# Fixed engine orders: evacuations of scores alternate with copies of the next unit's transposes, and GpSimd casts the first q

## The chip, the cores and the metric

One core of one Trainium2 chip. The metric is the device time of one execution in microseconds (us); lower is better. Ratios are the mean time of one kernel's fast runs over the mean of the other's fast runs of the same rounds, so they are not quite the ratio of the medians quoted beside them.

## The reference

```python
def setup_inputs():
    batch, heads, seq, dim = 8, 8, 512, 64     # q and k, float32, normal
def reference(q, k):
    scale = 1.0 / np.sqrt(q.shape[-1])
    return (np.einsum('bhqd,bhkd->bhqk', q, k) * scale).astype(np.float32)
```

Read 16.8 MB, write 67.1 MB. Everything between stays on the chip.

## The kernel before

The kernel works in 4 units of 2 batches. For a unit it loads k and q (one 2 MB transfer each), casts them to bf16, transposes them on PE in 8 tiles of 8 (128x128 blocks), and copies each transposed tile out of PSUM in four copies, tile by tile on VectorE or ScalarE. Then come 8 store tiles: in each, 4 times two matmuls of 512 columns and one evacuation (scaled, float32), alternately on ScalarE and VectorE; then one 2 MB store. The parts that the change touches:

```python
raw_pool = ... bufs=3      # loaded float32
bf_pool  = ... bufs=5      # cast
out_pool = ... bufs=4      # store tiles, 16 KB a partition
tpsum_pool = ... bufs=2    # transposed tiles, PSUM
psum_pool  = ... bufs=3    # scores, PSUM

def evacuate(dst, src):
    nonlocal n_evac
    if n_evac % 2 == 0:
        nc.scalar.mul(out=dst, in_=src, mul=scale)
    else:
        nc.vector.tensor_scalar(out=dst, in0=src, scalar1=scale, ...)
    n_evac += 1

# load_and_cast(v): two halves of k, then of q
                if v > 0:
                    copy = nc.gpsimd.tensor_copy
                else:
                    copy = (nc.vector.tensor_copy, nc.scalar.copy)[s]

# ... transpose(v, kb, qb) emits all 8 transposed tiles; scores(v, n, kT, qz) one store tile ...

cast = [load_and_cast(0)]
clear(nc.vector, qzs[0], 0)
clear(nc.gpsimd, qzs[0], 1)
for h in range(2):
    clear(nc.gpsimd, qzs[1], h)
for v in range(1, UNITS):
    cast.append(load_and_cast(v))

ts = {0: transpose(0, *cast[0])}
for v in range(UNITS):
    for n in range(N):
        scores(v, n, *ts[v])
        if n == (1 if v == 0 else N // 2 - 1) and v + 1 < UNITS:
            ts[v + 1] = transpose(v + 1, *cast[v + 1])
```

Nothing says in which order an engine runs the copies of the next unit and the evacuations of this one: a scheduler decides, and it runs the copies in a burst.

Of the kernel before, what the change touches and what calls it, by code (L numbers as in the profile page):

```python
# [1 line left out]

# [5 lines left out]


@with_exitstack  # L10
def kernel(
    ctx: ExitStack,
    tc: tile.TileContext,
    q: bass.AP,
    k: bass.AP,
    out: bass.AP,
):






    nc = tc.nc
    B, H, S, D = q.shape
    scale = 1.0 / (D ** 0.5)
    P = 128
    UNITS = B // 2
    N = H
    M = P // (2 * H)  # L30
    R = S // M
    J = R // 2
    RO = 8
    U = S // RO
    JJ = J // RO
    IW = 8 // JJ

    f32 = mybir.dt.float32
    bf16 = mybir.dt.bfloat16

    q_r = q.rearrange("(v b) g (m j) d -> v (b g m) (j d)", b=2, j=R)
    k_r = k.rearrange("(v b) g (m j) d -> v (b g m) (j d)", b=2, j=R)
    out_r = out.rearrange("(v b) (n h) (u i) k -> v (b n) (h u) (i k)", b=2, h=2, i=RO)

    consts = ctx.enter_context(tc.tile_pool(name="consts", bufs=1))
    raw_pool = ctx.enter_context(tc.tile_pool(name="raw", bufs=3))
    bf_pool = ctx.enter_context(tc.tile_pool(name="bf", bufs=5))
    t_pool = ctx.enter_context(tc.tile_pool(name="t", bufs=2))
    out_pool = ctx.enter_context(tc.tile_pool(name="out", bufs=4))
    tpsum_pool = ctx.enter_context(tc.tile_pool(name="tpsum", bufs=2, space=bass.MemoryType.PSUM))  # L50
    psum_pool = ctx.enter_context(tc.tile_pool(name="psum", bufs=3, space=bass.MemoryType.PSUM))

    n_evac = 0
    n_tp = 0

    def evacuate(dst, src):
        nonlocal n_evac
        if n_evac % 2 == 0:
            nc.scalar.mul(out=dst, in_=src, mul=scale)  # L59
        else:  # L60
            nc.vector.tensor_scalar(out=dst, in0=src, scalar1=scale, scalar2=None,  # L61
                                    op0=mybir.AluOpType.mult)
        n_evac += 1

    def half(h):
        return slice(h * D, (h + 1) * D)

    def load_and_cast(v):

        both = []  # L70
        for src in (k_r, q_r):
            xf = raw_pool.tile([P, 2, J * D], f32, name="xf")
            nc.sync.dma_start(out=xf, in_=src[v])
            xb = bf_pool.tile([P, J, 2, D], bf16, name="xb")
            for s in range(2):
                if v > 0:
                    copy = nc.gpsimd.tensor_copy
                else:
                    copy = (nc.vector.tensor_copy, nc.scalar.copy)[s]
                copy(out=xb[:, :, s, :], in_=xf[:, s].rearrange("p (j d) -> p j d", j=J))  # L80
            both.append(xb)
        return both

    def clear(engine, qz, h):

        engine.memset(qz[half(h), :, :, (1 - h) * U:(2 - h) * U], 0.0)  # L86

    def rearrange(tp, pattern, dst):

        nonlocal n_tp  # L90
        copy = (nc.vector.tensor_copy, nc.scalar.copy)[n_tp % 2]
        n_tp += 1
        for s in range(2):
            src = tp[half(s)].rearrange(pattern, n=N, h=2)
            for h in range(2):
                copy(out=dst(s, h), in_=src[:, h])  # L96

    def transpose(v, kb, qb):

        kT = t_pool.tile([P, N, M, 2, J], bf16, name="kT")  # L100
        qz = qzs[v % 2]
        for j0 in range(0, J, 8):
            tp = tpsum_pool.tile([P, 8, P], bf16, name="tp")
            for j in range(8):
                nc.tensor.transpose(out=tp[:, j, :], identity=identity,  # L105
                                    in_=kb[:, j0 + j].rearrange("p s d -> p (s d)"))
            rearrange(tp, "d j (n h m) -> d h n m j",
                      lambda s, h: kT[half(h), :, :, s, j0:j0 + 8])
        for i0 in range(0, RO, IW):
            tp = tpsum_pool.tile([P, IW, JJ, P], bf16, name="tp")  # L110
            for i in range(IW):
                for jj in range(JJ):
                    nc.tensor.transpose(out=tp[:, i, jj, :], identity=identity,  # L113
                                        in_=qb[:, RO * jj + i0 + i].rearrange("p s d -> p (s d)"))
            rearrange(tp, "d i jj (n h m) -> d h i n m jj",
                      lambda s, h: qz[half(h), i0:i0 + IW, :, h * U:(h + 1) * U]
                      .rearrange("d i n (m s jj) -> d s i n m jj", s=2, jj=JJ)[:, s])
        return kT, qz

    def scores(v, n, kT, qz):  # L120

        o = out_pool.tile([P, RO, S], f32, name="o")
        for i in range(0, RO, 2):
            ps = psum_pool.tile([P, 2, S], f32, name="ps")
            for w in range(2):
                nc.tensor.matmul(out=ps[:, w, :], lhsT=qz[:, i + w, n, :],  # L126
                                 rhs=kT[:, n].rearrange("d m s j -> d (m s j)"),
                                 start=True, stop=True)
            evacuate(o[:, i:i + 2, :], ps)
        nc.sync.dma_start(out=out_r[v, n], in_=o.rearrange("p i k -> p (i k)"))  # L130

    cast = [load_and_cast(0)]
    identity = consts.tile([P, P], dtype=bf16)
    make_identity(nc, identity)
    qzs = [consts.tile([P, RO, N, P], bf16, name=f"qz{n}") for n in range(2)]
    clear(nc.vector, qzs[0], 0)
    clear(nc.gpsimd, qzs[0], 1)
    for h in range(2):
        clear(nc.gpsimd, qzs[1], h)
    for v in range(1, UNITS):  # L140
        cast.append(load_and_cast(v))

    ts = {0: transpose(0, *cast[0])}
    for v in range(UNITS):
        for n in range(N):
            scores(v, n, *ts[v])
            if n == (1 if v == 0 else N // 2 - 1) and v + 1 < UNITS:
                ts[v + 1] = transpose(v + 1, *cast[v + 1])


# [1 line left out]
_INS = ['q', 'k']  # L152
_OUTS = [((8, 8, 512, 512), 'float32')]


# [23 lines left out]
```

## Time and profile before

| | before |
|---|---|
| time, median (range) | 204.84 us (204.29 to 205.01) |
| span of the profiled execution | 202.4 us |
| VectorE, ScalarE, PE busy | 63%, 52%, 53% |
| bytes | 83.9 MB, 415 GB/s over the span |

The groups of instructions give the durations that the prediction counts with (line, engine, operation, output<-input, shapes, count | busy us, mean ns | idle before, and its main releaser). An evacuation is 1.22 us on VectorE and 1.02 on ScalarE, a quarter of a transposed tile 0.69 and 0.58:

```profile
L61 DVE TENSOR_SCALAR o<-ps 128x1024 f32<-128x1024 f32 x64 | 77.7, 1223 | 41.0 <-DMA out_dram<-o 24.5
L59 ACT ACTIVATE o<-ps 128x1024 f32<-128x1024 f32 x64 | 62.9, 1022 | 49.3 <-DMA out_dram<-o 41.1
L96 DVE COPY qz<-tp 64x512 bf16<-64x512 bf16 x32 | 22.0, 688 | 6.5 <-PE tp L113 6.1
L96 ACT COPY qz<-tp 64x512 bf16<-64x512 bf16 x32 | 18.5, 580 | 14.2 <-PE tp L113 13.8
```

The releaser of the evacuations' idle time is a store: both engines wait for output buffers still being sent. So for most of the time the engines wait for the transfers.

### The profile page before, as it was taken

The numbers are of one execution on the slowest core, as the hardware profiler recorded it, in microseconds if no ns is written. First come the engines' busy times: TensorE is split into PE (matmuls) and PEld (weight loads), VectorE is DVE, ScalarE is ACT, GpSimd is POOL, SyncE is SP. The second block draws the span as 40 slices with busy tenths as digits, with TensorE's granted clock in tenths as the row PEclk, the third lists the DMA queues.
The fourth block names the chain that finished last, engine by engine and source line by source line (L and its number), as shares of the span: only waits on it lengthen the run. The fifth ranks groups of instructions, "written<-read, shape, count | busy, mean of one in ns | idle before, by whom it ended". The sixth has DMA issues, their size and how long they took to land. (4 is left out here: it accounts for less than half of the span.)

```text
span 202.4 us, 1541 instructions
## 1 busy us (share of the span) xinstructions
PE 106.3 (53%) x512; PEld 49.1 (24%) x512; DVE 128.5 (63%) x131; ACT 104.6 (52%) x131; POOL 33.6 (17%) x21
## 2 busy tenths in 40 slices
PE   0033468646646664788846573975565557452000
PEld 0033344324212323442213341321121222110000
DVE  3277768999855987669849986874444444444000
ACT  2218768997444586377659468653333333333000
POOL 8933777556000000000000000000000000000000
PEclk9999999999997958669988968896979755975555
DMA  6999999999999999999999999999999999999994
GB/s 207 437 437 421 434 437 421 415 411 431 440 421 434 428 424 431 434 395 415 418 418 428 440 418 415 431 444 421 421 418 447 424 415 418 444 434 415 423 447 191
DMA packets 5767, 83.98 MB, mean 415 GB/s; under 512 B 640, under 2 KB 640, under 8 KB 640
## 3 DMA queue, kind: packets, MB, share of 16 engines
q1 hardware_dynamic: 5760, 83.89, 97.9%
q8 instruction: 4, 0.07, 0.1%
q14 instruction: 3, 0.02, 0.0%
HBM read 16.78 MB, written 67.11 MB: 415 GB/s over the span
## 5 line engine op out<-in xcount | busy, mean ns | idle before, releaser
L126 PE MATMUL ps<-kT,qz 128*128 128x512 bf16 x256 | 84.8, 464 | 45.7 <-ACT o L59 38.6
L61 DVE TENSOR_SCALAR o<-ps 128x1024 f32<-128x1024 f32 x64 | 77.7, 1223 | 41.0 <-DMA out_dram<-o 24.5
L59 ACT ACTIVATE o<-ps 128x1024 f32<-128x1024 f32 x64 | 62.9, 1022 | 49.3 <-DMA out_dram<-o 41.1
L126 PEld LDWEIGHTS <-qz 128*128 128x128 bf16 x256 | 28.4, 113 | 94.0 <-issue 79.9
L96 DVE COPY qz<-tp 64x512 bf16<-64x512 bf16 x32 | 22.0, 688 | 6.5 <-PE tp L113 6.1
L96 ACT COPY qz<-tp 64x512 bf16<-64x512 bf16 x32 | 18.5, 580 | 14.2 <-PE tp L113 13.8
L105 PE MATMUL tp<-identity,xb 128*128 128x128 bf16 x128 | 12.1, 250 | 24.4 <-DVE xb L80 13.1
L80 POOL CAST xb<-xf 128x2048 bf16<-128x2048 f32 x12 | 22.4, 1896 | 14.5 <-DMA xf<-in_k_dram 9.8
L96 DVE COPY kT<-tp 64x512 bf16<-64x512 bf16 x32 | 22.0, 688 | 2.8 <-PE tp L105 2.3
L96 ACT COPY kT<-tp 64x512 bf16<-64x512 bf16 x32 | 18.5, 579 | 8.7 <-PE tp L105 8.2
L105 PEld LDWEIGHTS <-xb 128*128 128x128 bf16 x128 | 10.0, 113 | 28.6 <-issue 23.8
L113 PE MATMUL tp<-identity,xb 128*128 128x128 bf16 x128 | 12.5, 268 | 7.9 <-DVE kT L96 4.3
L113 PEld LDWEIGHTS <-xb 128*128 128x128 bf16 x128 | 11.3, 126 | 11.8 <-issue 8.8
L86 POOL MEMSET qz<- 64x4096 bf16 x3 | 10.5, 3508 | 0.1
L80 DVE CAST xb<-xf 128x2048 bf16<-128x2048 f32 x2 | 5.6, 2781 | 5.6 <-DMA xf<-in_k_dram 5.6
L80 ACT CAST xb<-xf 128x2048 bf16<-128x2048 f32 x2 | 3.8, 1898 | 6.6 <-DMA xf<-in_k_dram 6.6
L86 DVE MEMSET qz<- 64x2048 uint32 x1 | 1.8, 1765 | 1.2 <-PEq L163 1.2
L80 ACT ACT_TABLE_LOAD x1 | 1.3, 1283 | 0.7 <-PEq L163 0.7
masks.py:199 POOL TENSOR_SCALAR_AFFINE_SELECT identity<-identity 128x128 bf16<-128x128 bf16 x1 | 0.3, 293 | 0.1
masks.py:197 POOL MEMSET identity<- 128x128 bf16 x1 | 0.2, 205 | 0.3 <-POOLq L163 0.3
L163 POOL MEMSET const-float32-0.0<- 128x1 f32 x1 | 0.1, 104 | 0.2 <-issue 0.2
L163 POOL MEMSET const-bfloat16-1.0<- 128x1 bf16 x1 | 0.1, 112 | 0.0
(2 smaller groups left out, 0.2 us busy)
## 6 DMA issues: line engine op xcount, KB each, us to landing
out_dram<-o SPq DMA_DIRECT2D x32, 2048.0 KB, 15.9
xf<-in_k_dram SPq DMA_DIRECT2D x4, 2048.0 KB, 10.9
xf<-in_q_dram SPq DMA_DIRECT2D x4, 2048.0 KB, 11.6
```

Source lines behind the costliest of these rows:

```text
L59: nc.scalar.mul(out=dst, in_=src, mul=scale)
L61: nc.vector.tensor_scalar(out=dst, in0=src, scalar1=scale, scalar2=None, op0=mybir.AluOpType.mult)
L80: copy(out=xb[:, :, s, :], in_=xf[:, s].rearrange("p (j d) -> p j d", j=J))
L86: engine.memset(qz[half(h), :, :, (1 - h) * U:(2 - h) * U], 0.0)
L96: copy(out=dst(s, h), in_=src[:, h])
L105: nc.tensor.transpose(out=tp[:, j, :], identity=identity, in_=kb[:, j0 + j].rearrange("p s d -> p (s d)"))
L113: nc.tensor.transpose(out=tp[:, i, jj, :], identity=identity, in_=qb[:, RO * jj + i0 + i].rearrange("p s d -> p (s d)"))
L126: nc.tensor.matmul(out=ps[:, w, :], lhsT=qz[:, i + w, n, :], rhs=kT[:, n].rearrange("d m s j -> d (m s j)"), start=True, stop=True)
L163: nc = _bacc.Bacc("TRN2", target_bir_lowering=False, num_devices=1)
```

## The change

Its intent: copies of the next unit no longer come in a burst that holds up stores, and GpSimd, freed of the memsets (which VectorE takes), does the cast of the first q in place of the two engines that have to copy. Each instruction named is kept in program order on its engine, and `transpose` and `scores` become generators that are stepped in turn. The diff, cut to its core (the same wrapper is put around the transposes, matmuls, copies and casts):

```diff
+    pinned = tc.keep_in_program_order
     def evacuate(dst, src):
-            nc.scalar.mul(out=dst, in_=src, mul=scale)
+            pinned(nc.scalar.mul(out=dst, in_=src, mul=scale))
 ...
-                if v > 0:
-                    copy = nc.gpsimd.tensor_copy
-                else:
-                    copy = (nc.vector.tensor_copy, nc.scalar.copy)[s]
+                if v == 0 and src is k_r:
+                    copy = (nc.vector.tensor_copy, nc.scalar.copy)[s]
+                else:
+                    copy = nc.gpsimd.tensor_copy
 ...
-    def clear(engine, qz, h):
-        engine.memset(qz[...], 0.0)
+    def clear(qz, h):
+        nc.vector.memset(qz[...], 0.0)
 ...
             for h in range(2):
-                copy(out=dst(s, h), in_=src[:, h])
+                pinned(copy(out=dst(s, h), in_=src[:, h]))
+                yield
 ...
+    def take(steps, count):
+        for _ in range(count):
+            next(steps, None)
 ...
     for v in range(UNITS):
+        ahead = transpose(v + 1, *cast[v + 1]) if v + 1 < UNITS else iter(())
+        per_step = 3 if v == 0 else 1
         for n in range(N):
-            scores(v, n, *ts[v])
-            if n == (1 if v == 0 else N // 2 - 1) and v + 1 < UNITS:
-                ts[v + 1] = transpose(v + 1, *cast[v + 1])
+            take(ahead, 1)
+            for _ in scores(v, n):          # yields after each evacuation
+                take(ahead, per_step)
```

A unit's transposition has 40 steps (8 tiles, each one step of transposes and four of copies), and a store tile takes 5, so from unit 1 on each store tile carries one transposed tile.

More of the change, by code (lines that the diff above doesn't have):

```diff
@@ L58, in evacuate @@
         if n_evac % 2 == 0:
-            nc.scalar.mul(out=dst, in_=src, mul=scale)
+            pinned(nc.scalar.mul(out=dst, in_=src, mul=scale))
         else:
-            nc.vector.tensor_scalar(out=dst, in0=src, scalar1=scale, scalar2=None,
-                                    op0=mybir.AluOpType.mult)
+            pinned(nc.vector.tensor_scalar(out=dst, in0=src, scalar1=scale, scalar2=None,
+                                           op0=mybir.AluOpType.mult))
         n_evac += 1
@@ L75, in load_and_cast @@
             for s in range(2):
-                if v > 0:
+                if v == 0 and src is k_r:
+                    copy = (nc.vector.tensor_copy, nc.scalar.copy)[s]
+                else:
                     copy = nc.gpsimd.tensor_copy
-                else:
-                    copy = (nc.vector.tensor_copy, nc.scalar.copy)[s]
-                copy(out=xb[:, :, s, :], in_=xf[:, s].rearrange("p (j d) -> p j d", j=J))
+                pinned(copy(out=xb[:, :, s, :], in_=xf[:, s].rearrange("p (j d) -> p j d", j=J)))
             both.append(xb)
         return both
-    def clear(engine, qz, h):
-        engine.memset(qz[half(h), :, :, (1 - h) * U:(2 - h) * U], 0.0)
+    def clear(qz, h):
+        nc.vector.memset(qz[half(h), :, :, (1 - h) * U:(2 - h) * U], 0.0)
     def rearrange(tp, pattern, dst):
@@ L101, in transpose @@
         qz = qzs[v % 2]
+        ts[v] = (kT, qz)
         for j0 in range(0, J, 8):
@@ L104, in transpose @@
             for j in range(8):
-                nc.tensor.transpose(out=tp[:, j, :], identity=identity,
-                                    in_=kb[:, j0 + j].rearrange("p s d -> p (s d)"))
-            rearrange(tp, "d j (n h m) -> d h n m j",
-                      lambda s, h: kT[half(h), :, :, s, j0:j0 + 8])
+                pinned(nc.tensor.transpose(out=tp[:, j, :], identity=identity,
+                                           in_=kb[:, j0 + j].rearrange("p s d -> p (s d)")))
+            yield
+            yield from rearrange(tp, "d j (n h m) -> d h n m j",
+                                 lambda s, h: kT[half(h), :, :, s, j0:j0 + 8])
         for i0 in range(0, RO, IW):
@@ L112, in transpose, with scores @@
                 for jj in range(JJ):
-                    nc.tensor.transpose(out=tp[:, i, jj, :], identity=identity,
-                                        in_=qb[:, RO * jj + i0 + i].rearrange("p s d -> p (s d)"))
-            rearrange(tp, "d i jj (n h m) -> d h i n m jj",
-                      lambda s, h: qz[half(h), i0:i0 + IW, :, h * U:(h + 1) * U]
-                      .rearrange("d i n (m s jj) -> d s i n m jj", s=2, jj=JJ)[:, s])
-        return kT, qz
-    def scores(v, n, kT, qz):
+                    pinned(nc.tensor.transpose(out=tp[:, i, jj, :], identity=identity,
+                                               in_=qb[:, RO * jj + i0 + i].rearrange("p s d -> p (s d)")))
+            yield
+            yield from rearrange(tp, "d i jj (n h m) -> d h i n m jj",
+                                 lambda s, h: qz[half(h), i0:i0 + IW, :, h * U:(h + 1) * U]
+                                 .rearrange("d i n (m s jj) -> d s i n m jj", s=2, jj=JJ)[:, s])
+    def scores(v, n):
+        kT, qz = ts[v]
         o = out_pool.tile([P, RO, S], f32, name="o")
@@ L125, in scores @@
             for w in range(2):
-                nc.tensor.matmul(out=ps[:, w, :], lhsT=qz[:, i + w, n, :],
-                                 rhs=kT[:, n].rearrange("d m s j -> d (m s j)"),
-                                 start=True, stop=True)
+                pinned(nc.tensor.matmul(out=ps[:, w, :], lhsT=qz[:, i + w, n, :],
+                                        rhs=kT[:, n].rearrange("d m s j -> d (m s j)"),
+                                        start=True, stop=True))
             evacuate(o[:, i:i + 2, :], ps)
-        nc.sync.dma_start(out=out_r[v, n], in_=o.rearrange("p i k -> p (i k)"))
-    cast = [load_and_cast(0)]
+            yield
+        src = o.rearrange("p i k -> p (i k)")
+        nc.sync.dma_start(out=out_r[v, n], in_=src)
+    def take(steps, count):
+        for _ in range(count):
+            next(steps, None)
     identity = consts.tile([P, P], dtype=bf16)
@@ L135 @@
     qzs = [consts.tile([P, RO, N, P], bf16, name=f"qz{n}") for n in range(2)]
-    clear(nc.vector, qzs[0], 0)
-    clear(nc.gpsimd, qzs[0], 1)
-    for h in range(2):
-        clear(nc.gpsimd, qzs[1], h)
-    for v in range(1, UNITS):
-        cast.append(load_and_cast(v))
-    ts = {0: transpose(0, *cast[0])}
+    for qz in qzs:
+        for h in range(2):
+            clear(qz, h)
+    cast = [load_and_cast(v) for v in range(UNITS)]
+    ts = {}
+    for _ in transpose(0, *cast[0]):
+        pass
     for v in range(UNITS):
+        ahead = transpose(v + 1, *cast[v + 1]) if v + 1 < UNITS else iter(())
+        per_step = 3 if v == 0 else 1
         for n in range(N):
-            scores(v, n, *ts[v])
-            if n == (1 if v == 0 else N // 2 - 1) and v + 1 < UNITS:
-                ts[v + 1] = transpose(v + 1, *cast[v + 1])
+            take(ahead, 1)
+            for _ in scores(v, n):
+                take(ahead, per_step)
+        for _ in ahead:
+            pass
 _INS = ['q', 'k']
```

## The prediction

> **What bounds the kernel now.** I read the profile page first, then busy time by stage, then the store issues one by one. The page says that no compute engine is near full while the DMA engines are:
>
> ```profile
> PE 106.3 (53%) x512; PEld 49.1 (24%) x512; DVE 128.5 (63%) x131; ACT 104.6 (52%) x131; POOL 33.6 (17%) x21
> DMA  6999999999999999999999999999999999999994
> q1 hardware_dynamic: 5760, 83.89, 97.9%
> HBM read 16.78 MB, written 67.11 MB: 415 GB/s over the span
> ```
>
> VectorE is busy 63% of the span and the DMA row is at its top digit in every slice but the first and the last. The chain of waits that ended last is no use for finding a gain here: its largest member is "DMA out_dram<-o" at 22% of the span, which is each evacuation waiting for an output buffer still being stored, that is, the full queue again. So the question is only where the transfers are not flowing. Busy time by stage answers it (columns: stretch in us, its length, busy us of PE, PEld, DVE, ACT, POOL, granted clock, DMA share, GB/s); the stretches were cut where I had seen the share change:
>
> ```profile
> 0.00:1.50 1.50, 0.00 (x0) 0.00 (x0) 0.27 (x1) 0.76 (x1) 0.91 (x6) 1.00 0.00 0
> 4.00:34.00 30.00, 12.32 (x93) 9.06 (x94) 19.31 (x21) 16.04 (x21) 19.74 (x11) 1.00 1.01 433
> 34.00:44.00 10.00, 6.55 (x51) 3.52 (x50) 9.84 (x13) 9.33 (x14) 6.70 (x4) 1.00 1.00 413
> 60.00:90.30 30.30, 19.64 (x101) 10.26 (x101) 22.36 (x26) 18.31 (x26) 0.00 (x0) 0.73 1.01 429
> 90.30:91.50 1.20, 1.20 (x5) 0.40 (x4) 0.76 (x2) 1.02 (x1) 0.00 (x0) 0.78 0.33 137
> 91.50:200.00 108.50, 57.72 (x210) 21.69 (x209) 61.54 (x58) 49.44 (x57) 0.00 (x0) 0.76 1.00 426
> ```
>
> Loads run at 433 GB/s and stores at 426 to 429, with a share of 1.0. Half-microsecond windows swing between about 0.5 and 1.2, but they average to 1.0 over a few microseconds, so that is bookkeeping and not idling. There is one real hole, 90.3 to 91.5 us: share 0.33, so 1.2 x 0.67 = 0.8 us lost. The rest of the loss is 1.5 us before the first byte and about 2.4 us after the last (share 0.05 from 200.0 on).
>
> Why the hole? The time from a store's issue to its landing is a gauge of how much lies in the queue ahead of it. These are the three store issues before the hole (start, duration) and the one in it, each with its own line of DMA issues (last column: us to landing):
>
> ```profile
> 67.44 0.33 SPq L130 DMA_DIRECT2D out_dram<-o  x1
> out_dram<-o SPq DMA_DIRECT2D x1, 2048.0 KB, 16.3
> 74.91 0.33 SPq L130 DMA_DIRECT2D out_dram<-o  x1
> out_dram<-o SPq DMA_DIRECT2D x1, 2048.0 KB, 13.7
> 82.76 0.33 SPq L130 DMA_DIRECT2D out_dram<-o  x1
> out_dram<-o SPq DMA_DIRECT2D x1, 2048.0 KB, 10.8
> 90.76 0.33 SPq L130 DMA_DIRECT2D out_dram<-o  x1
> out_dram<-o SPq DMA_DIRECT2D x1, 2048.0 KB, 7.6
> ```
>
> A store of 2.097 MB at 427 GB/s takes 4.9 us. The last one met an empty queue, so 7.6 is 4.9 of transfer and 2.7 of fixed cost. The first had 16.3 - 7.6 = 8.7 us queued ahead. The next three intervals are 7.5, 7.8 and 8.0 us where the queue drains one store per 4.9: the deficit is 2.6 + 2.9 + 3.1 = 8.6 us, and the queue is dry. In that stretch both copying engines are in the burst of transposed copies for unit 2, with few evacuations between them. The next burst (for unit 3) does the same: stores issued at 112.4, 119.9 and 127.75 us land after 15.8, 13.1 and 10.2 us, so it ends 10.2 - 7.6 = 2.6 us short of dry. The first, during unit 0, is covered by loads.
>
> **What the Trainium skill says.** "DMA: Bandwidth & Descriptors", section "Where 436 GB/s comes from", puts the ceiling of a core's sixteen engines at 435.2 GB/s; the loads here run at 433 and the stores at 426 to 429, which agrees. "SBUF — State Buffer", section "The DMA setup-cost knee", gives every transfer a roughly fixed cost of about 2 us, mostly completion; my 2.7 us agrees roughly. The same page, section "SBUF: two separate sides", says that GpSimd and a VectorE operation in a two-port mode take one port pair as an exclusive lock, and the loser waits for the whole instruction. The trace agrees: VectorE's first cast starts at 8.63 us and takes 4.35 us, while GpSimd's memsets end at 11.90; 8.63 + 4.35 - 11.90 = 1.08 us, close to the 1.21 us that the second cast takes with GpSimd idle. "Perfetto Trace Analysis", section "Optimization Strategy", suggests interleaving regimes that are bound by different engines; that is this change, but it can only pay as much as the DMA engines idle.
>
> **The change part by part.** No transfer, matmul, copy or evacuation is added or removed: I compared instruction lists, and the queue of loads and stores has the same order and the same waits on buffers. What moves:
>
> 1. *Evacuations and copies alternate.* From unit 1 on, each of the 8 store tiles of a unit carries exactly one of the next unit's 8 transposed tiles, whose four copies run on one engine. On a VectorE turn VectorE does 4 x 0.688 + 2 x 1.223 = 5.2 us, on the other turn 2.45; ScalarE does 4 x 0.58 + 2 x 1.022 = 4.4 or 2.04 us. Over two tiles that is 7.65 us of VectorE and 6.4 of ScalarE against 9.8 us of DMA: 78% and 65%. A returned output buffer leaves three stores in the queue, 3 x 4.9 - 2.7 = 12 us before it is dry, and filling needs 5 to 6.5 us with some waits of one engine for the other. So the queue never empties: the hole of 0.8 us goes, and landings stay near 13 to 17 us in place of falling to 7.6. **Minus 0.8 us.**
>
> 2. *Unit 0 is denser: three steps after each evacuation.* 13 of the 40 steps fall in each store tile, so unit 1 is done in about three tiles. VectorE's share is 16 x 0.688 + 6 x 1.223 = 18.4 us, at least 6.1 us a tile. The loads keep the engines busy until about 2.6 + 8 x 4.9 = 42 us, so stores 1, 2 and 3 are wanted by about 41, 46 and 51 us. With the start below they come near 33, 39 and 45 us (before: 33.7, 36.1, 46.8). **0**, with 6 us to spare.
>
> 3. *The head.* Memsets: four on VectorE at 1.77 us (the one in this trace) from 1.24 us end near 8.3 us, just ahead of the first load's landing at 8.63. GpSimd is then free, so VectorE's first cast is no longer locked out: 1.21 us in place of 4.35, and ScalarE's 1.90 us sets the end, at 10.6 us. Transposes start about 2.5 us sooner than at 13.1. The first q lands at 1.19 + 12.3 = 13.5 us; GpSimd's two casts of 1.9 us end at 17.3, and the transposes want it at about 18.4 (before, 9.0 us after the first transpose; here less the 1.2 us of VectorE's cast, counted from 10.6). So the first evacuation comes near 26.6 us in place of 30.3. But all eight loads stand ahead of the first store in SyncE's order, and the eighth waits for a raw buffer whose cast ends near 32 us because its load lands only then. **0**: the earlier start buys slack and no time.
>
> 4. *The tail* is unchanged, the last four stores being queued back to back: **0**.
>
> Sum: 204.9 - 0.8 = 204.1 us.
>
> **The rivals.**
>
> *Fixed orders bring a new wait.* An engine that may not pass a copy waiting for its transposes holds up evacuations, so stores come later. For it speaks that two transpose buffers and three score buffers couple PE, VectorE and ScalarE closely, and that a VectorE turn at 5.2 us is already over the 4.9 us of a store. Against it, the turns alternate and the average is under 80%. To cost 2%, 4.1 us, the stores would have to fall 12 + 4 us behind within one run of tiles. A milder case reopens a hole of 1 us at a unit's boundary: 204.9 to 206.
>
> *GpSimd's cast of the first q is late.* It costs 3.8 us where the two engines took 1.9 side by side, and my slack is only 1 us. But another 5 us would still leave the first store inside the time that loads cover: no change.
>
> *The head start is worth its 3 to 4 us.* This would be so if compute were the bound early on, giving about 201 us. Against it: the share is 1.01 from 4 to 34 us, so the queue was not waiting for anything then.
>
> *The rate itself moves.* With 79 MB to pass after the head, 1% of rate is 2 us. The 34 to 44 us stretch, where loads and stores mix, ran at 413; a longer mix would cost 3% of it, 0.3 us. Even 433 GB/s throughout would make the stores' 67.1 MB only about 2 us shorter. No part of the change aims at this, but it sets the width of the range.
>
> **Range and chances.** The three runs before spread by 0.7 us (204.29 to 205.01). With plus or minus 0.4 for that and 0.5 for the rate, 203.2 to 205.2 should hold. Faster by 2% needs 200.8 us: closing the hole, and in addition 3 us from a head that bytes already fill. 2%. Slower by 2% needs 209 us, with VectorE or ScalarE behind for tens of microseconds: 3%. The rest is within 2%.
>
> **What would show it.** Right: a share of 1.0 in every stretch of several microseconds between 4 and 199 us with no second hole, landings of stores after about 60 us never below 12 us, store issues about 4.9 us apart in the middle, transposes starting near 10.6 us and the first VectorE cast at 1.2 us, the same 8-load order, stores' GB/s still 425 to 430. Step 1 is wrong if a store lands in under 10 us in units 1 to 3; step 3 is wrong if the first load lands later than 8.7 us or the span shrinks with the earlier start. The prediction as a whole fails if GB/s in full stretches differs from 427 by over 1%, or if evacuations show long waits for transposes with the DMA share below 0.9 beside them.

## The result, and the profile after

The changed kernel takes 204.06 us (203.96 to 204.42), before 204.84; ratio 0.9969, 95% interval 0.9947 to 0.9992. By the 2% measure it is the same; the small gain is clear of zero. The predicted 204.1 is met. How it came about is another matter, and the traces show a good part of it.

First what was foreseen. Busy time by stage in the kernel before, for the stretch around the hole and for the last transfers (columns as in the prediction: the last two are DMA share and GB/s):

```profile
88.00:92.00 4.00, 4.00 (x15) 1.56 (x13) 2.17 (x3) 2.80 (x4) 0.00 (x0) 0.65 0.84 356
196.00:200.00 4.00, 0.00 (x0) 0.00 (x0) 0.00 (x0) 0.00 (x0) 0.00 (x0) 0.50 0.92 393
```

and in the changed kernel:

```profile
88.00:92.00 4.00, 2.07 (x13) 1.34 (x12) 3.02 (x4) 2.29 (x3) 0.00 (x0) 0.79 1.02 434
196.00:200.00 4.00, 0.00 (x0) 0.00 (x0) 0.00 (x0) 0.00 (x0) 0.00 (x0) 0.50 0.55 233
```

The hole is gone. Two store issues of the changed kernel from the same part, each with its line of DMA issues (us to landing last), answer to those the prediction shows; there the landing fell to 7.6:

```profile
83.16 0.33 SPq L140 DMA_DIRECT2D out_dram<-o  x1
out_dram<-o SPq DMA_DIRECT2D x1, 2048.0 KB, 15.4
87.17 0.33 SPq L140 DMA_DIRECT2D out_dram<-o  x1
out_dram<-o SPq DMA_DIRECT2D x1, 2048.0 KB, 16.2
```

From 60 us on no store lands in under 15.3 us, and between 73 and 146 us issues alternate about 4.0 and 5.7 us apart. By the prediction's gauge there are never less than 15.3 - 7.6 = 7.7 us of work queued ahead. (The gauge's zero of 7.6 us is too high, as the completion times below show; the order of its readings stays right.)

Now what was not foreseen. The span of the profiled execution is 202.3 us against 202.4. The 0.8 us did not come out at the end. The second line of each pair shows where they went: in the last four microseconds the kernel before has its DMA engines at 92%, the changed one at 55%. Most of the sixteen engines are done early, and a few are not. The page's row of DMA shares says the same in its last digit, 4 before and 1 after, with a share of the queue no larger:

```profile
DMA  6999999999999999999999999999999999999991
q1 hardware_dynamic: 5760, 83.89, 97.7%
```

The trace also records, for each transfer, the times of its sixteen completions, one for each engine. It doesn't say which engine a completion belongs to; below, "the fastest" and "the slowest engine" are the first and the last of the sixteen. The transfers are counted with the eight loads, so the 18th is the tenth store. For three of the forty, first, eighth and last of the sixteen (us on the clock of the other views; the last column is a kernel with the transfers alone, told below):

```
transfer    before                  changed                 transfers alone
18th        90.83  91.15  93.51     90.89  91.14  93.64     90.92  91.29  91.77
19th        96.86  96.99  98.37     95.76  96.00  98.52     95.79  96.15  96.64
40th       199.97 200.09 201.53    197.98 198.40 201.48    198.12 198.25 198.74
```

By 90 us the slowest engine is 2.7 us behind the fastest in both kernels. In the kernel before, the fastest needs 6.03 us from the 18th transfer to the 19th, that is, 1.17 us more than its usual 4.86. The slowest needs 4.86: whichever engine was last at the 18th had finished the 19th by 98.37 us, so it did not idle. It was still busy with old work when the late store arrived. So the hole of the kernel before only made the fast engines wait for the slow one, and without it they keep their lead, 3.5 us at the end. The mean engine ends 1.45 us sooner (198.89 against 200.34 us), the last one 0.05. Only half of the 1.45 us comes at the hole; the rest is a slower pace after it, 4.92 us a transfer on average against 4.88, for which no run shows the cause. That the last completions agree so closely is partly chance: from the 18th transfer to the 40th the slowest engine loses about 1 us against 22 steps of 4.86 in either kernel, but in other places (22nd and 32nd transfer before, 34th to 38th in the changed one).

The same times correct the prediction's gauge. The store issued at 90.76 us did not meet an empty queue: the slowest engine had old work until 93.51 us, and 4.86 us later, at 98.37, the store had landed. So the 7.6 us are 2.75 of arrears and 4.86 of transfer. What an empty queue looks like is shown by a store of `burst` (an experiment below), issued after a stretch, 98.6 to 101.7 us, in which the DMA share was 0.00:

```profile
101.75 0.33 SPq L140 DMA_DIRECT2D out_dram<-o  x1
out_dram<-o SPq DMA_DIRECT2D x1, 2048.0 KB, 6.3
```

The zero of the gauge is 6.3 us and the fixed cost 6.3 - 4.9 = 1.4, not 7.6 and 2.7. And the gauge reads the slowest engine; the fastest runs dry sooner, by the spread between them.

The timed executions say it too. Each has its span besides its time, so the time can be split; means over the fast runs of one set of rounds (the changed kernel run again, 5 runs, the kernel before 9):

| | time | span | outside the span |
|---|---|---|---|
| before | 204.52 | 202.51 | 2.01 |
| changed | 204.14 | 202.36 | 1.78 |
| difference | -0.38 | -0.15 | -0.23 |

The traces show what goes with the part outside. On the queue q14, of kind instruction, most kernels still have a packet or two of 8 KB after the span's end. For the profiled executions (us):

| | outside the span | last q14 packet ends, after the span's end |
|---|---|---|
| before | 1.80 | 2.03 |
| deep_out | 1.87 | 2.10 |
| before, again | 2.14 | 2.37 |
| head_only | 2.38 | 2.62 |
| changed, both traces | 1.78, 1.80 | 1.16, 1.14 |
| the other fixed orders | 1.77 to 1.78 | 0.78 to 1.16 |
| transfers alone or with PE | 1.77 to 1.78 | none |

Where the packet ends before about 1.2 us, 1.77 to 1.80 us lie outside; in the four traces where it ends later, the time ends 0.23 to 0.24 us ahead of the packet's end each time. So what lies outside goes, in the profiled executions, with an instruction packet at the end of the program, and not with the transfers of data. No experiment moved that packet on purpose. The first row is the profiled execution of the first set, which took 204.16 us: in it the kernel before had hardly any surplus outside. The 0.15 us of span are small too: the kernel before has mean spans of 202.40 to 202.51 us in the other rounds, the changed one 202.36.

### The profile page after: what moved, and what is told of

Its sections match the earlier page's. It is cut to its first block, busy times and chain, and to the rows that moved or that the text cites. A ratio compares the mean times of both kernels' runs of the same rounds, so it can differ in the third digit from the quotient of the medians.

```text
span 202.3 us, 1549 instructions
## 1 busy us (share of the span) xinstructions
PE 106.1 (52%) x512; PEld 50.2 (25%) x512; DVE 129.6 (64%) x133; ACT 102.5 (51%) x130; POOL 26.8 (13%) x20
## 4 chain that ended last, share of the span: by engine, by line
DMA 52%; ACT 13%; DVE 13%; PE 10%; issue 2%; ACTq 0%; DVEq 0%; SPq 0%
DMA out_dram<-o 52%; ACT o L62 6%; DVE o L64 5%; PE ps L134 5%; ACT qz L99 4%; DVE qz L89 3%; ACT kT L99 3%; PE tp L120 3%; DVE kT L99 3%; PE tp L111 2%; DVE xb L83 1%; DVE qz L99 1%; ACTq L62 0%; DVEq L64 0%; SPq L140 0%
## 5 line engine op out<-in xcount | busy, mean ns | idle before, releaser
L134 PE MATMUL ps<-kT,qz 128*128 128x512 bf16 x256 | 87.3, 470 | 52.4 <-ACT o L62 43.3
L134 PEld LDWEIGHTS <-qz 128*128 128x128 bf16 x256 | 28.6, 115 | 98.6 <-issue 87.2
L83 POOL CAST xb<-xf 128x2048 bf16<-128x2048 f32 x14 | 26.1, 1893 | 21.5 <-DMA xf<-in_q_dram 18.1
L111 PE MATMUL tp<-identity,xb 128*128 128x128 bf16 x128 | 13.0, 267 | 17.0 <-DVE xb L83 11.1
L120 PE MATMUL tp<-identity,xb 128*128 128x128 bf16 x128 | 13.3, 271 | 8.1 <-ACT qz L99 4.9
L111 PEld LDWEIGHTS <-xb 128*128 128x128 bf16 x128 | 11.2, 122 | 21.3 <-ACT xb L83 11.1
L120 PEld LDWEIGHTS <-xb 128*128 128x128 bf16 x128 | 11.5, 123 | 12.6 <-issue 9.7
L89 DVE MEMSET qz<- 64x2048 uint32 x4 | 7.1, 1765 | 2.6 <-issue 1.4
L83 ACT CAST xb<-xf 128x2048 bf16<-128x2048 f32 x1 | 1.9, 1898 | 6.7 <-DMA xf<-in_k_dram 6.7
L83 DVE CAST xb<-xf 128x2048 bf16<-128x2048 f32 x1 | 1.2, 1227 | 0.0
```

What stands on the lines that cost most here:

```text
L83: pinned(copy(out=xb[:, :, s, :], in_=xf[:, s].rearrange("p (j d) -> p j d", j=J)))
L89: nc.vector.memset(qz[half(h), :, :, (1 - h) * U:(2 - h) * U], 0.0)
L111: pinned(nc.tensor.transpose(out=tp[:, j, :], identity=identity, in_=kb[:, j0 + j].rearrange("p s d -> p (s d)")))
L120: pinned(nc.tensor.transpose(out=tp[:, i, jj, :], identity=identity, in_=qb[:, RO * jj + i0 + i].rearrange("p s d -> p (s d)")))
L134: pinned(nc.tensor.matmul(out=ps[:, w, :], lhsT=qz[:, i + w, n, :], rhs=kT[:, n].rearrange("d m s j -> d (m s j)"), start=True, stop=True))
```

## The experiments

All ran on the same chip type, with the kernel before in each set of rounds. Times are medians; span is the mean of the same runs, and "outside" the mean of time less span. All runs are fast but one of the four of `burst`; its three fast runs alone have a median of 211.28 and a mean span of 209.63.

| kernel | time, us | ratio to before, 95% | span | outside |
|---|---|---|---|---|
| changed, again | 204.16 | 0.9980 (0.9968 to 0.9993) | 202.36 | 1.78 |
| order_only | 204.41 | 0.9993 (0.9979 to 1.0006) | 202.64 | 1.76 |
| head_only | 204.86 | 1.0016 (1.0003 to 1.0028) | 202.48 | 2.39 |
| deep_out | 204.24 | 0.9989 (0.9977 to 1.0002) | 202.46 | 1.87 |
| before, again | 204.50 | 1.0001 (0.9988 to 1.0013) | 202.42 | 2.05 |
| burst | 212.01 | 1.034 (1.0294 to 1.0386) | 210.15 | 1.78 |
| late1 | 204.14 | 0.9983 (0.9969 to 0.9996) | 202.32 | 1.78 |
| late4 | 210.68 | 1.0303 (1.0287 to 1.0319) | 208.88 | 1.78 |
| dma_only | 201.35 | 0.9844 (0.9831 to 0.9858) | 199.55 | 1.80 |
| dma_pe | 203.48 | 0.9944 (0.9931 to 0.9958) | 201.66 | 1.79 |
| dma_only_hole | 201.40 | 0.9846 (0.9831 to 0.9860) | 199.58 | 1.79 |
| dma_pe_hole | 203.43 | 0.9948 (0.9934 to 0.9961) | 201.62 | 1.79 |

**The two kernels again.** No edit. Two theories stood: the prediction's (the hole's mean share is the gain) and the drift (the slowest engine did not idle in it).

> The changed kernel once more, for a tighter interval and a second trace. Theory (the hole of 0.8 us mean is what went): 0.3 to 0.4% faster than the kernel before, 203.9 to 204.4 us. Rival (the slowest DMA engine never idled in that hole, because the engines have drifted 2.7 us apart by then, so removing it buys little and the measured 0.3% is luck of the runs): ratio 0.999 to 1.001. In the trace both expect no hole in mid-kernel and the last of the sixteen completions of each transfer about 2.8 us behind the first.

> The kernel before against itself: the ratio's interval must hold 1 and shows what 5 rounds can tell apart, some 0.1 to 0.2%. A second trace: theory says that the hole near 90 us is there again, with three stores landing in ever shorter times ahead of it, because it follows from the order of instructions and not from chance.

The changed kernel is 0.2% faster, 0.38 us in the means, and the kernel before against itself gives 1.0001. So a gain is there; it is half of 0.8 us, and of that half only 0.15 us lies in the span. The second trace of the changed kernel ends as the first did, with 3.6 us between the sixteen completions of the last transfer. The second trace of the kernel before has the hole at the same store (it lands after 7.6 us), but shallower: the store was issued at 89.93 us instead of 90.76, the fastest engine lost 0.35 us and the slowest 0.03. So the hole varies from run to run, and in neither trace did the slowest engine lose time in it. (There its arrears were 1.8 us and not 2.7.)

**The alternation alone** (`order_only`):

```diff
-                if v == 0 and src is k_r:
+                if v == 0:
                     copy = (nc.vector.tensor_copy, nc.scalar.copy)[s]
 ...                                    # and three of four memsets back on GpSimd
```

> The fixed alternation alone: the first q is cast by VectorE and ScalarE and three of the four memsets are on GpSimd, as before. The first transposed copies come about 3 us later than in the changed kernel, because the cast of q stands before them in the fixed order. Theory (alternation gives all the gain, the head gives none): the same time as the changed kernel within 0.15%, no hole after 60 us; the third store comes about 3 us later than 48.2 us, just inside its slack of 3.8 us. Rival (the head's earlier start gives it): the same time as the kernel before.

204.41 us: 0.12% above the changed kernel, inside what was expected, but all five runs lie above all five of the changed kernel, so with a fixed order the kernel with the old head is about 0.25 us slower. Against the kernel before, the ratio's interval contains 1: the alternation alone was not shown to gain any time, and the rival is not excluded by the time. The hole is closed as well (no landing under 15.3 us after 66 us). The head is late for the reason that the change had in mind: the cast of q stands ahead of the copies in VectorE's order, and its first cast is locked out by GpSimd's memsets again. The first line is that cast in VectorE's timeline, the others the third store's issue:

```profile
8.39 4.58 DVE L83 CAST xb<-xf 128x2048 bf16<-128x2048 f32 x1 [5.39 <-DMA xf<-in_k_dram]
50.35 0.33 SPq L140 DMA_DIRECT2D out_dram<-o  x1
out_dram<-o SPq DMA_DIRECT2D x1, 2048.0 KB, 8.5
```

The third store lands after 8.5 us, 2.2 over an empty queue for the slowest engine; the fastest is 1.9 us ahead of it, so without the new head the fixed order has almost no slack in unit 0. The 0.25 us do not lie in the transfers: in the trace the last completion comes as early as in the changed kernel (201.50 against 201.48 us), and the span ends 0.3 us later after it, because the closing steps (DRAIN) of ScalarE and VectorE start at 202.19 and 202.29 us and not at 201.88 and 201.90. Why they do is open.

**The head alone** (`head_only`):

```diff
-                if v > 0:
+                if v > 0 or src is q_r:
 ...
-    clear(nc.gpsimd, qzs[0], 1)
+    clear(nc.vector, qzs[0], 1)         # and the two of qzs[1]
```

> The head alone: GpSimd casts the first q and VectorE does all memsets, the scheduler's order of copies and evacuations stays. Theory: the hole near 90 us stays, because the burst of copies for unit 2 is still there, and the time is that of the kernel before within 0.15%. Rival (head start matters): 0.3% faster.

The burst and its hole stay, as expected: the store at the same place lands after 7.6 us.

```profile
90.67 0.33 SPq L130 DMA_DIRECT2D out_dram<-o  x1
out_dram<-o SPq DMA_DIRECT2D x1, 2048.0 KB, 7.6
```

Here too the fastest engine idled (5.92 us from the 18th transfer to the 19th) and the slowest did not (4.88). The span is that of the kernel before (202.48 against 202.51). The time is 0.16% longer, and all of that lies outside the span: 2.39 us against 2.01, with the latest instruction packet of all traces. The rival (head start gives the gain) falls.

**The hole closed in another way** (`deep_out`), with the scheduler's burst kept:

```diff
-    bf_pool = ctx.enter_context(tc.tile_pool(name="bf", bufs=5))
+    bf_pool = ctx.enter_context(tc.tile_pool(name="bf", bufs=3))
-    out_pool = ctx.enter_context(tc.tile_pool(name="out", bufs=4))
+    out_pool = ctx.enter_context(tc.tile_pool(name="out", bufs=5))
```

> The kernel before with five output buffers in place of four and three buffers of cast inputs in place of five, to make room. The bursts of copies stay. Theory (the hole is the loss, and it came of the queue's depth against the burst): the queue is 4.9 us deeper, no store lands in under 12 us at the bursts, no hole, and the time is that of the changed kernel within 0.15%. Rival (the order of the instructions itself matters, or fixed orders do something else to the transfers): the time of the kernel before.

No store after 60 us lands in under 14.9 us, and 88 to 92 us has a share of 1.01. The queue's depth against the burst is thus what made the hole: order and depth are two cures for it. The time, in the means, is 0.09% above the changed kernel's, as expected, but also only 0.11% under the kernel before, with an interval that contains 1: the time tells neither theory from the other. The span is only 0.05 us under that of the kernel before, and the last completions are 3.8 us apart. This is the second kernel in which closing the hole hardly moved the span.

**A large hole on purpose** (`burst`):

```diff
-        per_step = 3 if v == 0 else 1
+        per_step = 3 if v == 0 else 0
 ...
-            take(ahead, 1)
+            take(ahead, 1 if v == 0 else 40 * (n == 3))
```

> The changed kernel with all 40 transposition steps of the next unit in one block ahead of the fourth store tile in units 1 and 2, in place of one step after each evacuation. The block lasts about 16.8 us (so long as unit 0's transposition took), so one store comes 16.8 + 2.5 = 19 us after the one ahead of it, 14.4 us over the pace of 4.9. With 8.7 us in the queue the theory expects a hole of about 5.5 us in each of the two units: 204.1 + 11 = 215 us, 5% slower. Rival (the transfers are the bound whatever the order, or the engines' drift takes up such holes): under 1% slower.

212.0 us; the four runs spread from 210.2 to 213.5. The store interval across the first block is 19.1 us (82.62 to 101.75), as expected. The profiled execution, which is the 213.5 and counts as slow beside the others, shows two unequal holes (busy time by stage, DMA share and GB/s last):

```profile
96.00:98.00 2.00, 1.85 (x5) 0.73 (x5) 1.94 (x4) 1.97 (x4) 0.00 (x0) 0.50 0.08 33
98.00:100.00 2.00, 1.07 (x4) 0.25 (x3) 1.16 (x1) 1.98 (x3) 0.00 (x0) 0.50 0.00 0
100.00:102.00 2.00, 2.00 (x6) 0.66 (x5) 1.23 (x1) 0.91 (x2) 0.00 (x0) 0.50 0.00 0
142.00:144.00 2.00, 1.51 (x6) 0.57 (x6) 1.12 (x2) 1.75 (x3) 0.00 (x0) 1.00 0.04 16
```

Some 6.4 us and 2.7 us of engine time are lost around them (the missing shares of 94 to 104 and of 142 to 146 us), 9.1 together, and this execution is 9.4 us above the changed kernel's median. The expected 11 was too much for the second block. The completion times tell what the mean hides. In the first hole the fastest engine's step is 12.11 us, 7.25 over its usual 4.86, and the slowest engine's is 9.51, only 4.65 over: it worked off its arrears of 2.8 us while the others waited, and the sixteen come out 0.2 us apart. In the second hole it is 3.4 us against 1.7. So the slowest engine idled 6.4 us and not 9.1. The rest comes back later: once the engines are level, the next long instruction packet (126.6 and 169.2 us in this trace) makes one of them the new slowest, with steps of 6.72 and 6.73 us, 1.9 over. By the number alone the mean share (9.1 for 9.4) does as well: for holes this long the two ways of counting come out alike, and this run does not choose between them. (The four runs' spread is not explained; one is slow, and of it only the shares and steps are read.)

**A later start** (`late1`, `late4`): the four copies of one transposed tile of unit 0 are done once or four times more on VectorE.

```diff
+            if v == 0 and i0 == RO - 2 * IW:
+                for _ in range(1):      # late4: range(4)
+                    ...                 # the tile's four copies on VectorE again
```

> The changed kernel with one set of four transposed copies of the first unit done twice on VectorE, so that everything after it starts about 2.4 us later. The gauge (time to landing less 7.6 us) gave the third store of the changed kernel 11.4 - 7.6 = 3.8 us of slack. Theory: no hole, the same time within 0.3%. Rival (an earlier start is worth its time): 2.4 us, 1.2% slower.

> The same with the four copies done five times, so a start about 10.8 us later. Theory: 10.8 less the slack of 3.8 gives a hole of 7 us near the third store, 211 us, 3.4% slower. If the prediction's own figure of 6 us to spare were right, 209 us. Rival (start counts in full): 215 us.

With `late1` stores 1, 2 and 3 are issued at 35.8, 43.5 and 50.1 us instead of 34.3, 40.8 and 48.2, and the time is the changed kernel's (204.14): the slack is real, and a start earlier by 2 us is worth nothing. With `late4` the third store comes 9.4 us later and the time rises by 6.5 us; 9.4 less 6.5 makes a slack of 2.9 us, not the 6 of the prediction. (The gauge's 3.8 used the zero of 7.6; with 6.3 it is 5.1 for the slowest engine, and 2.4 for the fastest, which is 2.7 us ahead.) The stage of its holes and what follows:

```profile
40.00:58.00 18.00, 12.69 (x73) 6.53 (x72) 17.66 (x22) 14.78 (x22) 5.54 (x3) 0.91 0.64 271
58.00:200.00 142.00, 80.34 (x349) 34.33 (x355) 91.65 (x90) 74.29 (x90) 0.00 (x0) 0.82 1.00 426
```

18 us at a share of 0.64 is 6.5 us lost, and 6.5 us is what the end shows. Here the slowest engine idled as well: the first late store's step is 8.56 us for it and 8.62 for the fastest, since the engines were still 0.9 us apart.

**The transfers alone, and beside PE** (`dma_only`, `dma_pe`; wrong results): the same 8 loads and 32 stores in the same order, the stores all from one tile of zeros; then the same with 512 matmuls and their weight loads on zeros, which wait for no transfer.

```diff
-    # casts, transposes, matmuls, evacuations
+    for v in range(UNITS):
+        for src in (k_r, q_r):
+            xf = raw_pool.tile([P, 2, J * D], f32, name="xf")
+            nc.sync.dma_start(out=xf, in_=src[v])
+    nc.vector.memset(o, 0.0)
+    # dma_pe only: 64 x 8 matmuls of 512 columns on zeros
+    for v in range(UNITS):
+        for n in range(N):
+            nc.sync.dma_start(out=out_r[v, n], in_=o)
```

> The same 8 loads and 32 stores and no computation: the stores all send one tile of zeros (wrong result on purpose). It is the floor of these transfers. Theory (the changed kernel keeps the transfers flowing from end to end): the floor is 0 to 0.7% below the changed kernel, 202.7 to 204.1 us. If it is under 200 us, something in the changed kernel still slows the transfers and the prediction's reading that the rate is the limit is incomplete.

> The same with 512 matmuls and their 512 weight loads on zeros, which wait for no transfer. In both traces so far four packets of 16 KB on the queue of kind instruction took 0.9 to 1.1 us each, beside the data's 0.61, at times when PE's instructions run on. Theory: those packets delay the engines that carry them by up to 1 us each, so this kernel ends 0.5 to 3 us after the one with transfers alone. Rival: the fetches do not show in the end, under 0.3 us.

The floor is 201.35 us, lower than expected: 2.8 us are left in the changed kernel, seven times what the change brought (0.38 us). And 2.1 of them come with 512 matmuls and their weight loads alone, which exchange no data with the transfers. The DMA row and the queue's share for the transfers alone, then the queues with PE:

```profile
DMA  6999999999999999999999999999999999999996
q1 hardware_dynamic: 5760, 83.89, 98.9%
```

```profile
q1 hardware_dynamic: 5760, 83.89, 97.9%
q8 instruction: 4, 0.07, 0.1%
```

The transfers alone end with all engines within 0.6 us of each other; with PE they end 2.9 us apart, the mean engine only 0.53 us later (198.85 against 198.32 us) and the last 2.30 (201.04 against 198.74). The four packets on the instruction queue are 0.1% of the traffic, 16 KB each, and take 0.88 to 1.10 us each where a data packet of that size takes 0.61. The slowest engine's steps from one transfer to the next show when it falls behind. In `dma_pe` the first such packet comes at 25.7 us, and the step from 23.1 to 29.5 us is 6.44 in place of 4.9. In the changed kernel it comes at 32.0 us and the step from 28.2 to 34.2 is 5.93; in the kernel before at 36.3, and the step from 33.1 to 38.9 is 5.78. In eleven of the twelve traces with PE's stream the first long step is that of the transfer in flight, or next to start, at this packet (in `late4` the packet falls into the hole; in `order_only` and the second trace of the kernel before it comes just ahead of the change from loads to stores, so two causes fall together there); in the two without PE there is none before the loads change to stores. At that change every engine loses about 0.5 us in `dma_only` (one step of 5.36), and the slowest engine of the other kernels mostly 0.9 to 1.3. The later packets mostly fall on engines with time to spare. Of the 2.30 us of `dma_pe`, 1.55 come at the first packet and 0.75 at the change from loads to stores (a step of 6.11 against 5.36), where there is no such packet; why the engine that is behind loses more there is open.

Is it the fetch, or PE's work? PE works from 5.5 to 117.6 us in `dma_pe`. The time that the sixteen engines lose there against `dma_only`, summed over them, is 1.5, 1.6, 1.9 and 1.4 us in the four transfers under way at the packets (25.7, 53.5, 81.2 and 109.1 us), 2.4 at the change, and under 0.4 in every other one. From 56 to 80 us, between two packets, PE is busy for 23.9 of 24 us and the transfers run at 431 GB/s. So PE's work as such doesn't slow the transfers here; the loss comes at the packets. No kernel with the same PE work and fewer instructions was run.

**A hole of known size, with and without the spread** (`dma_only_hole`, `dma_pe_hole`): one store held back by a chain of VectorE operations, meant to last until about 91 us (score buffers cut from 3 to 2 to make room for the chain's tile).

```diff
+    for c in range(66):
+        pinned(nc.vector.tensor_scalar(out=scratch[:, c % 4, :], in0=cps, ...))
+    pinned(nc.vector.tensor_copy(out=late[:, :128], in_=scratch[:, 1, :128]))
 ...
-            nc.sync.dma_start(out=out_r[v, n], in_=o)
+            nc.sync.dma_start(out=out_r[v, n], in_=late if (v, n) == (1, 2) else o)
```

> The transfers alone, with the eleventh store held back by a chain on VectorE until about 91 us (wrong result on purpose), which should leave the fastest DMA engine dry for about 1.4 us, like the hole of the kernel before. Here the sixteen engines are only 0.8 us apart, so none is far enough behind to fill its hole with old work. Both theories expect the hole in the end: 1.2 to 1.6 us above 201.35, so 202.6 to 203.0 us.

> The same hold-back, about 1.5 us for the fastest engine, beside the 512 matmuls (wrong result on purpose). In that kernel the slowest engine is 3 us behind the fastest at this time. Drift theory: the slowest engine still has old work when the held store arrives, never idles, and sets the end, so the time stays at 203.5 us, plus at most 0.2. Rival, as the prediction reckoned (time lost is the hole's mean share): about 1.3 us more, 204.8 us.

Both missed. The chain's 66 operations took 1.13 us each (74.8 us together), not the 1.22 of an evacuation, so the store was ready at 85.6 us and 85.9 us, before any queue was dry, and no share below 0.96 appears there. They test nothing about holes. They do repeat the pair above (201.40 and 203.43 us), with VectorE busy for 75 us beside the transfers at no cost. The drift's main claim, that the slowest engine sets the end and a short hole does not reach it, therefore rests on the completion times of three traces with the hole (`before`, `before_again`, `head_only`), and on the spans of `deep_out` and of the changed kernel. It was not tested with a hole of known size.

No version tried beats the changed kernel with a right result.

## Why the prediction was right, and where it was right by luck

**What bounds the kernel.** Right in kind, incomplete in degree. The transfers are the bound, and a GB/s of 426 to 433 with a share of 1.0 was read as the rate's limit, so that nothing but the hole was left to gain. `dma_only` shows 3.2 us under the kernel before. A mean share of 1.0 over sixteen engines does not show that one of them falls 2.7 us behind between 28 and 45 us.

**Step 1, the alternation.** The mechanism held: the hole closed, landings stayed at 15.3 us and above where 13 to 17 was forecast, and `deep_out` shows that depth against burst was its cause. The gauge was read with a wrong zero: 7.6 us was not "an empty queue" with 2.7 of fixed cost, but the slowest engine's arrears of 2.75 us and one transfer; an empty queue lands in 6.3 (`burst`). The agreement with the page's fixed cost of about 2 us was thus an agreement with something else. The size failed: minus 0.8 us was the hole's mean share times its length, and the span lost 0.15 us. The time is set by the slowest engine, which did not idle in the hole. The rule "share missing times length" holds where the hole is much longer than the spread of the engines (`late4`: 6.5 us lost, 6.5 us longer).

**Step 2, unit 0 denser.** No cost, right. But stores 2 and 3 came at 40.8 and 48.2 us, not 39 and 45, because 6.1 us a tile was VectorE's work alone and the engines also wait for one another (6.5 and 7.4 us measured). The third store of the changed kernel landed after 11.4 us:

```profile
48.24 0.33 SPq L140 DMA_DIRECT2D out_dram<-o  x1
out_dram<-o SPq DMA_DIRECT2D x1, 2048.0 KB, 11.4
```

So the slack was 2.9 us by `late4`, in place of 6.

**Step 3, the head.** No gain in time, right for the start as such, and shown by `head_only` (span) and `late1`. The prediction's own sign against it, a span that shrinks with the earlier start, did appear from `order_only` to the changed kernel (202.64 to 202.36 us), but in the trace it lies after the last completion. Its details, from the timelines of GpSimd and VectorE, before:

```profile
4.83 7.07 POOL L86 MEMSET qz<- 64x4096 bf16 x2
8.63 4.35 DVE L80 CAST xb<-xf 128x2048 bf16<-128x2048 f32 x1 [5.63 <-DMA xf<-in_k_dram]
```

and after:

```profile
7.91 1.76 DVE L89 MEMSET qz<- 64x2048 uint32 x1 [0.47 <-issue]
9.71 1.23 DVE L83 CAST xb<-xf 128x2048 bf16<-128x2048 f32 x1
13.58 3.73 POOL L83 CAST xb<-xf 128x2048 bf16<-128x2048 f32 x2 [12.28 <-DMA xf<-in_q_dram]
```

The lock-out of the first cast is gone (4.35 us to 1.23), and GpSimd's casts end at 17.3 us as forecast. The memsets end at 9.67 and not at 8.3, since 0.47 us of issue lie between them, so the first transpose starts at 11.1 us and not at 10.6. The first evacuation came at 29.8 us, not 26.6: the reckoning scaled the old chain, and in the new one PE waits for ScalarE's copies and transposes a tile of unit 1 ahead of the first matmul. Only 0.5 us of the forecast 3.7 us of head start were left. It cost nothing, because the head does not set the end.

**Step 4, the tail.** Called unchanged. It is not: the last four microseconds went from a share of 0.92 to 0.55. That is where step 1 disappeared: the fast engines end sooner, the slowest does not.

**The sum.** 204.1 was forecast and 204.06 measured. Against the kernel before in the same rounds the means differ by 0.38 us (5 and 9 runs) to 0.6 us (the first set, 4 runs each). In the set where the split is known, 0.15 of the 0.38 us lie in the span and 0.23 outside it, which the prediction did not consider. The part outside is 1.76 to 1.80 us on average in every kernel written in the fixed order or with the transfers alone, and 2.01 to 2.05, 1.87 and 2.39 in the three that the scheduler orders, the last with the new head. It goes with the end of the last instruction packet, as shown above; why that packet comes later in the scheduler's orders is open. That the number was met is luck twice over. The base of 204.9 was the median of three runs, and the kernel before has 204.41 to 204.57 in all later rounds; and of the gain of 0.8 us forecast for the hole only 0.15 appears in the span, the one set where it can be split.

**The rivals.** A new wait did not come up. The late cast did not matter. The head start in full was refuted. The rate moved a little: from 92 to 196 us it is 426 and 427 GB/s in the two traces of the kernel before and 430 in both of the changed one, inside the 1% that the prediction allowed. It does not follow the hole (427 in `order_only`, which has none), and its cause is open.

## What to carry to other kernels

When the transfers are the limit, read the time from a store's issue to its landing as a gauge of the queue: a fall by steps shows a burst of other work draining it, and either more buffers or an interleaved order stops it. But price a hole by the engine that ends last and not by the mean share: in these traces a hole shorter than the engines' spread cost the slowest engine next to nothing, and a longer one levelled the engines first. Take the gauge's zero from a store that met a queue shown to be empty. Split a small gain into span and the rest before explaining it. And run the transfers alone once: here that showed in one run that seven times the change's gain was left, on another path.

## What the Trainium skill lacked or had wrong

- "Runtime: NRT & Kernel Launch", section "Instruction fetch mechanics", says that crossing a 16 KiB instruction boundary is "mostly hidden". Beside transfers that fill the DMA engines it was not, for the transfers: four 16 KB instruction packets took 0.88 to 1.10 us each on the DMA engines (0.61 for data), each cost the engines 1.4 to 1.9 us in sum, and the first one 1.55 of the 2.30 us by which the last completion came later beside PE's stream than alone. The page does not speak of instruction packets after the program's span, which in four traces end 0.23 to 0.24 us after the measured time does.
- "DMA: Bandwidth & Descriptors", section "Where 436 GB/s comes from", has the sixteen engines and their common ceiling, but not that they drift apart within one core's stream of plain transfers: 0.6 to 0.9 us for the transfers alone, 2.5 to 3.6 us in the changed kernel after the loads. (The page's "Latency and other measured facts" does say that two of the engines are usually slower in traces; these traces do not name the engine.) The section that the prediction took 435.2 GB/s from also says that for transfers between HBM and SBUF a limit of about 358 GB/s a core binds; the loads here ran at 433 and the stores at 426 to 430, with one core at work.
- "SBUF — State Buffer", section "The DMA setup-cost knee", has about 2 us of fixed cost for a transfer; a store into an empty queue took 6.3 us here, 1.4 over the 4.9 us of its bytes.
- No page that I read prices a hole by the slowest engine (a hole of 0.8 us by the mean share was worth 0.15 us of span), or uses the time from issue to landing as a gauge of the queue (16.3 us with a full queue, 6.3 us with an empty one).
